# A two-layer hybrid backbone on one core: fold splits on VectorE, row copies first, the context's root inside the first product, and the order of the gate tiles

## The chip, the cores and the metric

The kernel runs on one core of a Trainium2 chip. The metric is the device time of one execution in microseconds, the median of several runs. A profile is one execution recorded by the hardware profiler; its span is the part of it between the first and the last instruction.

## The reference, cut to what matters

The network has two layers over 1024 latent tokens of width 1024; 256 context tokens only feed the recurrence of the first layer. The parts that the change touches stand at the very beginning of layer one, and in weights of layer two that are folded together ahead of time:

```python
shift, scale, gate = jnp.split(sc @ mod_w[l] + mod_b[l], 3, axis=-1)
hx = modulate(rmsnorm(x, norm_g[l]), shift[:, None], scale[:, None])
hc = modulate(rmsnorm(ctx, norm_g[l]), shift_c, scale_c)
...
xb_c = hc @ pe["w_in"][:, 3 * W_CONV:3 * W_CONV + W_LRU]
_, h_ctx = rglru_branch(xb_c, pe, h0, False)
out_x, _ = even_mixer(hx, h_ctx, pe)
```

`sc` is SiLU of the conditioning vector. `even_mixer` computes five products of `hx` (value va and gate vg of a convolution, ga, xb of the recurrence, gb). Layer two multiplies by a product of two weights (`od_w_in` and `od_w_grp`), which the kernel computes once: the "fold".

## The kernel before

All activations lie with channels on the 128 partitions, in eight tiles of 128 x 1024 (x_0 to x_7). Every product is made of float32r parts: an operand is split into a high part (a cast on ScalarE, "wh", "h0h", "cth") and a low part (source less high part, on VectorE or GpSimd, "wl", "h0l", "ctl"), and three matmuls replace one (high x high, high x low, low x high). `split` (line 102) and `wload` (line 123) do that for weights: a load into "wr", a cast into "wh", a subtraction into "wl", each with two buffers.

The beginning of the kernel, up to line 525, is one list of calls that is written out by hand. In it, loads (`load`, line 108) and matmuls (`mm`, line 117) are chained: each is issued after the one before it in the list. SP's queue thus takes the loads and the stores of the folds strictly in the written order, and a store that waits for its data holds back every load behind it. The other engines are ordered by a scheduler, within these chains and the data's dependences.

The list does these things, interleaved:

- `fold(g)` (line 250) for g = 0 and 1, as a generator that `fold_some` steps on. Each of its four parts takes a weight tile wu (through `weight`, line 254), makes 24 matmuls of 512 columns into two PSUM tiles, copies both into a tile fo on ScalarE, and puts a store of it on a list that `store_folds` (line 321) empties into SP's queue.
- The sum of squares of x, its root, spread over the partitions by a matmul (ms_x).
- The shift and scale of layer one, in four blocks b: `mod_loads` (line 374) multiplies four weight tiles (modw) by the conditioning into one PSUM row (modr), `mod_cols` (line 386) copies that row into SBUF on ScalarE (modrow) and turns it into columns by eight small matmuls (modt), which VectorE adds into m and a. `modulate(k)` (line 399) then scales tile x_k in place and splits it into h0h and h0l.
- The context: `ctx_load` (line 444) loads two tiles (cx) and sums their squares into ssqc, `ctx_scale` (line 452) takes the root (a matmul ms_c, a square root on ScalarE, a reciprocal on VectorE) and scales both tiles, `ctx_split` (line 458) modulates and splits them into cth and ctl.
- The gate of layer one: `spread_c` loads the conditioning onto all partitions (cL) and applies SiLU on ScalarE, and `gates(a, b)` (line 437) takes a weight tile each (mod) and forms its dot product with cL on VectorE.

Behind the list, the loop over j (line 770) runs the products of layer one in an order fixed by hand (`on`, line 530): xb_0 (lines 762 to 765, 48 matmuls, not chained to the list), then for j = 0 vg (48), the context's xbc (24 matmuls of 256 columns), va (48), the context's part for j = 1, and the recurrence's gate products g mixed with xb_1. The taps of a short convolution (uc), their split (uh, ul) and the products with the gates follow on VectorE, ScalarE and GpSimd. GpSimd makes the low parts of the weights in this loop (`raw_split`, line 565), after it has made those of three of the four tiles wu of fold 1.

Of the kernel before, what the change touches and what calls it, by code (L numbers as in the profile page):

```python
# [17 lines left out]
C = 256  # L18
E = C + S
D = 1024  # L20
KT = D // P
# [35 lines left out]
def body(ctx, tc, xT, ctxT, cc, ccol, modT, modW, win, gw, wout, wu, grp, wg, wo1, small, edge, ident, outT):  # L57
# [24 lines left out]
    def ttile(name):  # L82
        return tpool.tile([P, H], F32, tag="t", name=name)
# [8 lines left out]
    def wide(name):  # L92
        return pc.tile([P, S], F32, tag="xb", name=name)
# [33 lines left out]
    def wload(src, name, eng, n=D, out=None):  # L127
        raw = wpool.tile([P, n], F32, tag="wr", name=f"wr_{name}")
        load(raw, src)
        if out is None:  # L130
            hi = wpool.tile([P, n], F32R, tag="wh", name=f"wh_{name}")
            lo = wpool.tile([P, n], F32R, tag="wl", name=f"wl_{name}")
        else:
            hi, lo = out(f"wh_{name}", F32R), out(f"wl_{name}", F32R)
        split(raw, hi, lo, eng)
        return hi, lo


    def mm3_steps(ps, w, xs, cols, ks=KT):
        hi, lo = w  # L140
        xh, xl = xs
        for k in range(ks):
            kc = slice(k * P, (k + 1) * P)
            nc.tensor.matmul(ps, hi[:, kc], xh[k][:, cols], start=(k == 0), stop=False)  # L144
            nc.tensor.matmul(ps, hi[:, kc], xl[k][:, cols], start=False, stop=False)  # L145
            nc.tensor.matmul(ps, lo[:, kc], xh[k][:, cols], start=False, stop=(k == ks - 1))  # L146
            yield

    def mm3(ps, w, xs, cols, ks=KT):
# [48 lines left out]
    def rstd(acc, eps, name, wn=0):  # L198
        n = acc.shape[-1]
        ps = psum(f"ms_{name}") if n < H else banks(f"ms_{name}", wn)[0]  # L200
        nc.tensor.matmul(ps[:, :n], ones, acc, start=True, stop=True)
        rt = ttile(f"sq_{name}")
        nc.scalar.activation(rt[:, :n], ps[:, :n], AF.Sqrt, bias=eps)
        nc.vector.reciprocal(acc, rt[:, :n])
# [45 lines left out]
    def fold(g, raw_tile, out_tile, g_tile=None, w_tile=None):  # L250
        g_tile = g_tile or dtile
        gh, gl, early = [], [], None

        def weight(kp):
            return wload(wu[g, kp], f"wu_{g}_{kp}", nc.vector if g == 0 or kp == 0 else nc.gpsimd)

        for i in range(2):
            if w_tile is None and i == 1:
                early = weight(0)
            raw = raw_tile(f"graw_{g}_{i}")  # L260
            load(raw, grp[g, i])
            th = g_tile(f"gh_{g}_{i}", F32R)
            tl = g_tile(f"gl_{g}_{i}", F32R)
            split(raw, th, tl, nc.vector)
            gh += [th[:, 0:H], th[:, H:D]]
            gl += [tl[:, 0:H], tl[:, H:D]]
        yield
        if w_tile is not None:
            ws = [wload(wu[g, kp], f"wu_{g}_{kp}", nc.gpsimd, out=w_tile[kp]) for kp in range(KT // 2)]
            yield  # L270
        for kp in range(KT // 2):
            if w_tile is None:
                wh, wl = early
            else:
                wh, wl = ws[kp]
            if w_tile is None and kp + 1 < KT // 2:
                early = weight(kp + 1)
                yield
            pss = [psum(f"fold_{g}_{kp}_{s}") for s in range(2)]

            def terms(s):
                for i in range(4):
                    kc = slice(i * 2 * P + s * P, i * 2 * P + (s + 1) * P)
                    mm(pss[s], wh[:, kc], gh[i], start=(i == 0), stop=False)
                    mm(pss[s], wh[:, kc], gl[i], start=False, stop=False)
                    yield
                    mm(pss[s], wl[:, kc], gh[i], start=False, stop=(i == 3))
                    yield

            dst = wfold[g][:, :, 2 * kp : 2 * kp + 2, :]  # L290
            if w_tile is None:
                o = out_tile(f"fo_{g}_{kp}").rearrange("p (m s c) -> p m s c", s=2, c=P)
                todo = [terms(s) for s in range(2)]
                if (g, kp) == (0, 0):
                    for _ in range(2):
                        for t in todo:
                            for _ in range(4):
                                next(t)
                for s in range(2):
                    for _ in todo[s]:  # L300
                        pass
                    nc.scalar.copy(o[:, :, s, :], pss[s].rearrange("p (m c) -> p m c", c=P))
                    if s:
                        stores.append((dst.rearrange("m p s c -> p m (s c)"), o.rearrange("p m s c -> p m (s c)")))
                    yield
            else:
                for s in range(2):
                    for _ in terms(s):
                        pass
# [11 lines left out]
    def store_folds(n):  # L321
        while n and stores:
            load(*stores.pop(0))
            n -= 1
# [10 lines left out]
    with ExitStack() as sctx:  # L335
# [23 lines left out]
        def sumsq(acc_, v, n, first, name):  # L359
            if first:  # L360
                nc.scalar.activation(acc_[:, :n], v, AF.Square)
            else:
                q = ttile(name)
                nc.scalar.activation(q[:, :n], v, AF.Square)
                nc.vector.tensor_tensor(out=acc_[:, :n], in0=acc_[:, :n], in1=q[:, :n], op=add)


        idx = spool.tile([P, P], F32, name="idx")
# [5 lines left out]
        def mod_loads(b, qs):  # L374
            if b not in modr:
                modr[b] = psum(f"modr_{b}")
            for q in qs:
# [3 lines left out]
                for e in range(4):  # L381
                    mm(modr[b][32 * e : 32 * e + 32, j * MC : (j + 1) * MC], cpad[:, 4 * half + e],
                                     raw[:, e * MC : (e + 1) * MC], start=(q == 0), stop=(q == 3),
                                     skip_group_check=True)

        def mod_cols(b):
            row = ttile(f"modrow_{b}")
            nc.scalar.copy(row, modr[b])
# [55 lines left out]
        def ctx_load(i):  # L444
            cx.append(xtile(f"cx_{i}"))
            cth.append(ctile(f"cth{i}", F32R))
            ctl.append(ctile(f"ctl{i}", F32R))
            load(cx[i].rearrange("p (k n) -> p k n", n=C), ctxT[4 * i : 4 * i + 4].rearrange("k p n -> p k n"))
            for q4 in range(4):
                sumsq(accc, cx[i][:, q4 * C : (q4 + 1) * C], C, i + q4 == 0, f"csq_{i}_{q4}")  # L450

        def ctx_scale():
            rstd(accc, eps_r, "c")
# [30 lines left out]
        for _, roots in rx:  # L484
            roots()
        rx = [r for r, _ in rx]
        mod_cols(0)
        modulate(0)
        modulate(1)
        mod_loads(1, range(4))  # L490
        store_folds(2)
        fold_some(2)
        mod_cols(1)
# [1 line left out]
        modulate(3)  # L495
        fold_some(1)
        mod_loads(2, range(4))
        store_folds(1)
        fold_some(2)
        mod_cols(2)  # L500
        modulate(4)
        modulate(5)
        mod_loads(3, range(4))
        fold_some(1)
        mod_cols(3)
        modulate(6)
# [3 lines left out]
        fold_some(2)  # L510
        with tc.issue_after(last_low[0].ins), tc.issue_after(last_low[1].ins):
            ctx_load(0)
            ctx_load(1)
        w_vg0 = wload(win[KT], "vg0", nc.vector)
        store_folds(3)
        spread_c()
        gates(2 * KT, 2 * KT + 4)
        ctx_scale()
        ctx_split(0)
        ctx_split(1)  # L520
        raw_va0 = wpool.tile([P, D], F32, tag="wr", name="wr_va0")
        load(raw_va0, win[0])
        gates(2 * KT + 4, 2 * KT + 6)
        load(eg, edge)
        chained[0] = False


    last = {}

    def on(eng, f, *args, **kw):  # L530
        with ExitStack() as octx:
# [152 lines left out]
    with ExitStack() as actx:  # L684
# [77 lines left out]
        w = w_xb0  # L762
        xb = wide("xb0")
        for h in range(2):
            mm3(xb[:, HALF[h]], w, (hh, hl), HALF[h])
        xc = psum("xbc0")[:, :C]
        w = w_vg0
        uc = utile("uc0")
# [1095 lines left out]
```

## Time and profile before

| | |
|---|---|
| time, median of 3 runs | 1302.21 us (1300.24 to 1302.76) |
| the profiled execution | 1304.29 us, span 1302.4 us |
| mean granted TensorE clock | 0.991 |
| busy in the span: PE, DVE, ACT, POOL | 1268.6, 1135.5, 648.0, 296.3 us |
| PE busy from 60 to 70 us, and its clock | 8.72 of 10, 0.83 |
| PE busy from 90 to 100 us, and its clock | 6.32 of 10, 0.89 |
| PE busy from 100 to 110 us, and its clock | 9.60 of 10, 0.77 |

PE is TensorE's matmuls, PEld its weight loads, DVE is VectorE, ACT ScalarE, POOL GpSimd, SPq the queue that SP issues. A row of a timeline has the start, the length, the engine, the line, the operation, what it writes and reads, and in brackets the idle time of its engine ahead of it with what ended that. A row of a table by stretches has the stretch, its length, busy time and count of instructions of each engine, the granted clock, the share of time in which the DMA engines are busy, and GB/s.

### The profile page before, as it was taken

The numbers are of one execution on the slowest core, as the hardware profiler recorded it, in microseconds if no ns is written. First come the engines' busy times: TensorE is split into PE (matmuls) and PEld (weight loads), VectorE is DVE, ScalarE is ACT, GpSimd is POOL, SyncE is SP. The second block draws the span as 40 slices with busy tenths as digits, with TensorE's granted clock in tenths as the row PEclk, the third lists the DMA queues.
The fourth block names the chain that finished last, engine by engine and source line by source line (L and its number), as shares of the span: only waits on it lengthen the run. The fifth ranks groups of instructions, "written<-read, shape, count | busy, mean of one in ns | idle before, by whom it ended". The sixth has DMA issues, their size and how long they took to land.

```text
span 1302.4 us, 16089 instructions
## 1 busy us (share of the span) xinstructions
PE 1268.6 (97%) x5804; PEld 1042.2 (80%) x5804; DVE 1135.5 (87%) x1758; ACT 648.0 (50%) x937; POOL 296.3 (23%) x149
## 2 busy tenths in 40 slices
PE   9999999999999999999999999999999999999995
PEld 7678888888888887888887878887878888788784
DVE  6878899999999999968969969998999987887776
ACT  7543666566566633237535346633343434645442
POOL 0202644364535546443210022000000000000002
PEclk9998999999999999999999999999999999999997
DMA  9961111112111233442418565234333334868623
GB/s 367 385 212 41 57 54 53 57 57 73 39 67 57 70 127 120 156 143 90 155 40 298 172 209 175 93 122 154 120 115 114 113 121 141 295 226 278 227 78 129
DMA packets 78783, 182.33 MB, mean 140 GB/s; under 512 B 7664, under 2 KB 23408, under 8 KB 78704
## 3 DMA queue, kind: packets, MB, share of 16 engines
q1 hardware_dynamic: 70256, 177.12, 39.1%
q10 hardware_dynamic: 8448, 4.20, 1.1%
q8 instruction: 45, 0.74, 0.2%
q14 instruction: 34, 0.28, 0.1%
HBM read 137.24 MB, written 44.04 MB: 139 GB/s over the span
## 4 chain that ended last, share of the span: by engine, by line
PE 47%; DVE 29%; DMA 13%; ACT 4%; issue 4%; POOL 1%; SPq 0%; POOLq 0%; DVEq 0%; ACTq 0%
DVE conv L534 7%; PE wob L534 6%; PE va L534 5%; PE xb L534 4%; PE vg L534 4%; DVE l L534 3%; PE g L534 3%; DMA yr_t<-y_t 2%; DMA wr_wu<-wu 2%; PE ga L145 2%; PE ga L534 2%; PE ga L144 2%; PE ga L146 2%; PE xbc L534 2%; DVE ws L1401 1%
## 5 line engine op out<-in xcount | busy, mean ns | idle before, releaser
L534 DVE SCALAR_TENSOR_TENSOR conv<-u,sm,conv 128x505 f32<-128x505 f32 (+6 forms) x224 | 153.5, 745 | 1.0
L1683 POOL TENSOR_TENSOR o<-x,rr 128x256 f32<-128x256 f32 (+1 forms) x9 | 8.0, 927 | 454.0 <-ACT rr L1671 451.0
L534 ACT ACTIVATE l<-g,sm 128x512 f32<-128x512 f32 (+1 forms) x96 | 58.6, 618 | 57.8 <-PE g L534 57.0
L104 POOL TENSOR_TENSOR wl_wu<-wr_wu,wh_wu 128x1024 fp32r<-128x1024 f32 x11 | 26.3, 2393 | 160.0 <-ACT wh_wu L103 125.8
L123 PE MATMUL fold<-gh,wh_wu 128*128 128x512 f32 x128 | 51.7, 404 | 2.1 <-ACT wh_wu L103 2.1
L534 POOL TENSOR_TENSOR l<-l,l 128x1280 f32<-128x1280 f32 x16 | 47.1, 2962 | 25.6 <-DVE conv L534 14.0
L534 PE MATMUL wob<-ybl,wh_wob 128*128 128x512 f32 x128 | 50.1, 392 | 2.3 <-POOL ybl L534 2.3
L103 ACT CAST wq_g<-wr_g 128x512 fp32r<-128x512 f32 x48 | 28.2, 620 | 47.2 <-DMA wr_g<-wg 15.6
L123 PE MATMUL fold<-gh,wl_wu 128*128 128x512 f32 x128 | 50.7, 398 | 0.5 <-DVE wl_wu L104 0.5
L123 PE MATMUL fold<-gl,wh_wu 128*128 128x512 f32 x128 | 50.6, 395 | 0.2 <-DVE gl L104 0.2
L534 PE MATMUL va<-h0h,wh_va 128*128 128x512 f32 x128 | 50.2, 392 | 0.0
L534 PE MATMUL gb<-h0h,wl_gb 128*128 128x512 f32 x128 | 49.9, 390 | 0.2 <-POOL wl_gb L534 0.2
L534 PE MATMUL va<-h0l,wh_va 128*128 128x512 f32 x128 | 50.0, 391 | 0.0
L534 PE MATMUL va<-h0h,wl_va 128*128 128x512 f32 x128 | 50.0, 391 | 0.0
L534 PE MATMUL wob<-ybh,wl_wob 128*128 128x512 f32 x128 | 49.8, 389 | 0.0
L534 PE MATMUL gb<-h0h,wh_gb 128*128 128x512 f32 x128 | 49.8, 389 | 0.0
L534 PE MATMUL gb<-h0l,wh_gb 128*128 128x512 f32 x128 | 49.8, 389 | 0.0
L534 PE MATMUL vg<-h0h,wl_vg 128*128 128x512 f32 x128 | 49.8, 389 | 0.0
L534 PE MATMUL vg<-h0l,wh_vg 128*128 128x512 f32 x128 | 49.8, 389 | 0.0
L534 PE MATMUL wob<-ybh,wh_wob 128*128 128x512 f32 x128 | 49.8, 389 | 0.0
L534 PE MATMUL vg<-h0h,wh_vg 128*128 128x512 f32 x128 | 49.8, 389 | 0.0
L534 DVE TENSOR_TENSOR_SCAN l<-l,l 128x256 f32<-128x256 f32 (+1 forms) x32 | 48.7, 1522 | 1.1
(593 smaller groups left out, 4303.8 us busy)
## 6 DMA issues: line engine op xcount, KB each, us to landing
wr_wu<-wu SPq DMA_DIRECT2D x16, 512.0 KB, 4.9
modw<-modW SPq DMA_DIRECT2D x16, 512.0 KB, 10.2
x_part<-xp SPq DMA_DIRECT2D x32, 256.0 KB, 2.2
mod<-modT SPq DMA_DIRECT2D x32, 256.0 KB, 3.8
wr_v<-wfold SPq DMA_DIRECT2D x16, 512.0 KB, 4.0
wr_g<-wg SPq DMA_DIRECT2D x16, 512.0 KB, 5.0
wr_wo<-wo SPq DMA_DIRECT2D x16, 512.0 KB, 4.7
yr_t<-y_t SPq DMA_DIRECT2D x16, 512.0 KB, 6.2
```

The source lines that it names most:

```text
L103: return (nc.scalar.copy(hi, src), eng.tensor_tensor(out=lo, in0=src, in1=hi.bitcast(F32), op=sub))
L104: eng.tensor_tensor(out=lo, in0=src, in1=hi.bitcast(F32), op=sub))
L123: m = nc.tensor.matmul(*args, **kw)
L144: nc.tensor.matmul(ps, hi[:, kc], xh[k][:, cols], start=(k == 0), stop=False)
L145: nc.tensor.matmul(ps, hi[:, kc], xl[k][:, cols], start=False, stop=False)
L146: nc.tensor.matmul(ps, lo[:, kc], xh[k][:, cols], start=False, stop=(k == ks - 1))
L534: last[eng] = f(*args, **kw)
L1401: nc.vector.tensor_tensor(out=nxt[:, :, a_:b_], in0=cur[:, :, a_ + o0 : b_ + o0], in1=cur[:, :, a_ + o1 : b_ + o1], op=add)
L1683: nc.gpsimd.tensor_tensor(out=o[:, k - k0], in0=v, in1=rr, op=mult)
```

## The change

Five edits, all in the first 110 us of the kernel. The three low parts of fold 1's weights move from GpSimd to VectorE. The row copy of `mod_cols` gets a call of its own (`mod_row`), which stands right behind its matmuls; for block 3 it is also put ahead of `modulate(4)`. In the list, one of the three last stores of the folds goes behind the conditioning, two gate tiles and va's weight. Two of the six gate products stand ahead of the context's root, bound behind its last sum of squares, and four behind the last split of the context. And xb_0 is now chained to the list: its first 12 of 16 steps stand ahead of the root's matmul, 4 behind it.

```diff
         def weight(kp):
-            return wload(wu[g, kp], f"wu_{g}_{kp}", nc.vector if g == 0 or kp == 0 else nc.gpsimd)
+            return wload(wu[g, kp], f"wu_{g}_{kp}", nc.vector)
...
+        rows = {}
+
+        def mod_row(b):
+            rows[b] = ttile(f"modrow_{b}")
+            return nc.scalar.copy(rows[b], modr[b])
+
         def mod_cols(b):
-            row = ttile(f"modrow_{b}")
-            nc.scalar.copy(row, modr[b])
+            row = rows[b]
...
         mod_cols(2)
-        modulate(4)
+        mod_loads(3, range(4))
+        with tc.issue_after(mod_row(3).ins):
+            modulate(4)
         modulate(5)
-        mod_loads(3, range(4))
...
             ctx_load(0)
-            ctx_load(1)
+            squares = ctx_load(1)
         w_vg0 = wload(win[KT], "vg0", nc.vector)
-        store_folds(3)
+        store_folds(2)
         spread_c()
-        gates(2 * KT, 2 * KT + 4)
-        ctx_scale()
-        ctx_split(0)
-        ctx_split(1)
+        with tc.issue_after(squares.ins):
+            gates(2 * KT, 2 * KT + 2)
         raw_va0 = wpool.tile([P, D], F32, tag="wr", name="wr_va0")
         load(raw_va0, win[0])
-        gates(2 * KT + 4, 2 * KT + 6)
+        store_folds(1)
+        xb0 = wide("xb0")
+        first = (x for h in range(2) for x in mm3_steps(xb0[:, HALF[h]], w_xb0, (hh, hl), HALF[h], KT, mm))
+        for _ in range(KT + 4):
+            next(first)
+        ctx_scale()
+        for _ in first:
+            pass
+        ctx_split(0)
+        with tc.issue_after(ctx_split(1)[1].ins):
+            gates(2 * KT + 2, 2 * KT + 6)
         load(eg, edge)
         chained[0] = False
 
-    last = {}
+    last = {"pe": pe[0]}
```

The same is done in `rstd` (its matmul goes through `mm`), and lines 762 to 765 go.

On ScalarE, around the row copy of block 3 (modrow of modr_699 before, of modr_687 now); h0h_689 and h0h_716 are the high part of x_4, the next one that of x_5, wh_xb the cast of xb_0's weight. Before:

```order
L103 COPY wh_wu_3_656<-wr_wu_3_654 128x1024
L302 COPY fo_2_662<-fold_2_0_660 128x4x128
L406 ACTIVATE h0h_689<-x_290,m_132 128x1024
L406 ACTIVATE h0h_695<-x_412,m_132 128x1024
L388 COPY modrow_737<-modr_699 128x512
L103 COPY wh_xb_762<-wr_xb_760 128x1024
```

And now:

```order
L103 COPY wh_wu_3_658<-wr_wu_3_656 128x1024
L302 COPY fo_2_664<-fold_2_0_662 128x4x128
L390 COPY modrow_712<-modr_687 128x512
L411 ACTIVATE h0h_716<-x_290,m_132 128x1024
L411 ACTIVATE h0h_722<-x_412,m_132 128x1024
L103 COPY wh_xb_762<-wr_xb_760 128x1024
```

The row copy moved ahead of both high parts.

On VectorE, from the last sum of squares of the context to its second low part ctl_812; mod_16 and the following are the gate tiles, uc the first tap behind xb_0. Before:

```order
L365 TENSOR_TENSOR ssqc<-ssqc,csq_3_823 128x256
L441 TENSOR_SCALAR mod_16_837,m_132<-mod_16_837,cL 128x1024
L441 TENSOR_SCALAR mod_17_840,m_132<-mod_17_840,cL 128x1024
L204 RECIPROCAL ssqc<-sq_c 128x256
L441 TENSOR_SCALAR mod_18_843,m_132<-mod_18_843,cL 128x1024
L441 TENSOR_SCALAR mod_19_846,m_132<-mod_19_846,cL 128x1024
L456 TENSOR_TENSOR cx_796<-cx_796,ssqc 128x1024
L456 TENSOR_TENSOR cx_810<-cx_810,ssqc 128x1024
L441 TENSOR_SCALAR mod_20_870,m_132<-mod_20_870,cL 128x1024
L415 TENSOR_SCALAR cx_796<-cx_796,a_133,m_132 128x256 x4
L441 TENSOR_SCALAR mod_21_873,m_132<-mod_21_873,cL 128x1024
L415 TENSOR_SCALAR cx_810<-cx_810,a_133,m_132 128x256 x4
```

And now, from the second gate product on:

```order
L446 TENSOR_SCALAR mod_17_839,m_132<-mod_17_839,cL 128x1024
L204 RECIPROCAL ssqc<-sq_c 128x256
L463 TENSOR_TENSOR cx_796<-cx_796,ssqc 128x1024
L463 TENSOR_TENSOR cx_810<-cx_810,ssqc 128x1024
L420 TENSOR_SCALAR cx_796<-cx_796,a_133,m_132 128x256 x4
L420 TENSOR_SCALAR cx_810<-cx_810,a_133,m_132 128x256 x4
L104 TENSOR_TENSOR ctl_798<-cx_796,cth_797 128x1024
L104 TENSOR_TENSOR ctl_812<-cx_810,cth_811 128x1024
L446 TENSOR_SCALAR mod_18_913,m_132<-mod_18_913,cL 128x1024
L446 TENSOR_SCALAR mod_19_916,m_132<-mod_19_916,cL 128x1024
L446 TENSOR_SCALAR mod_20_919,m_132<-mod_20_919,cL 128x1024
L446 TENSOR_SCALAR mod_21_922,m_132<-mod_21_922,cL 128x1024
```

Four gate products left the context's chain and stand between it and the taps uc.

On ScalarE, the end of the context's chain: csq are its squares, cL the conditioning's SiLU, cth the high parts, wh_va the cast of va's weight. Now:

```order
L302 COPY fo_3_769<-fold_3_1_768 128x4x128
L103 COPY wh_vg_828<-wr_vg_826 128x1024
L440 ACT_TABLE_LOAD
L440 ACTIVATE cL<-cL 128x1024
L364 ACTIVATE csq_1_817<-cx_810 128x256
L364 ACTIVATE csq_2_820<-cx_810 128x256
L364 ACTIVATE csq_3_823<-cx_810 128x256
L203 ACT_TABLE_LOAD
L203 ACTIVATE sq_c<-ms_c,eps_r 128x256
L103 COPY cth_797<-cx_796 128x1024
L103 COPY cth_811<-cx_810 128x1024
L553 COPY wh_va_975<-wr_va_842 128x1024
```

Before, cL and its table load stood behind the last three squares, and wh_va, a convolution tap, a table load and a sigmoid stood between the two cth.

More of the change, by code (lines that the diff above doesn't have):

```diff
@@ L136, in wload, with mm3_steps @@
         return hi, lo
-    def mm3_steps(ps, w, xs, cols, ks=KT):
+    def mm3_steps(ps, w, xs, cols, ks=KT, mm=nc.tensor.matmul):
         hi, lo = w
@@ L143, in mm3_steps @@
             kc = slice(k * P, (k + 1) * P)
-            nc.tensor.matmul(ps, hi[:, kc], xh[k][:, cols], start=(k == 0), stop=False)
-            nc.tensor.matmul(ps, hi[:, kc], xl[k][:, cols], start=False, stop=False)
-            nc.tensor.matmul(ps, lo[:, kc], xh[k][:, cols], start=False, stop=(k == ks - 1))
+            mm(ps, hi[:, kc], xh[k][:, cols], start=(k == 0), stop=False)
+            mm(ps, hi[:, kc], xl[k][:, cols], start=False, stop=False)
+            mm(ps, lo[:, kc], xh[k][:, cols], start=False, stop=(k == ks - 1))
             yield
@@ L200, in rstd @@
         ps = psum(f"ms_{name}") if n < H else banks(f"ms_{name}", wn)[0]
-        nc.tensor.matmul(ps[:, :n], ones, acc, start=True, stop=True)
+        mm(ps[:, :n], ones, acc, start=True, stop=True)
         rt = ttile(f"sq_{name}")
@@ L364, in sumsq @@
                 nc.scalar.activation(q[:, :n], v, AF.Square)
-                nc.vector.tensor_tensor(out=acc_[:, :n], in0=acc_[:, :n], in1=q[:, :n], op=add)
+                return nc.vector.tensor_tensor(out=acc_[:, :n], in0=acc_[:, :n], in1=q[:, :n], op=add)
         idx = spool.tile([P, P], F32, name="idx")
@@ L449, in ctx_load @@
             for q4 in range(4):
-                sumsq(accc, cx[i][:, q4 * C : (q4 + 1) * C], C, i + q4 == 0, f"csq_{i}_{q4}")
+                d = sumsq(accc, cx[i][:, q4 * C : (q4 + 1) * C], C, i + q4 == 0, f"csq_{i}_{q4}")
+            return d
         def ctx_scale():
@@ L486, in body @@
         rx = [r for r, _ in rx]
+        mod_row(0)
         mod_cols(0)
@@ L490, in body @@
         mod_loads(1, range(4))
+        mod_row(1)
         store_folds(2)
@@ L497, in body @@
         mod_loads(2, range(4))
+        mod_row(2)
         store_folds(1)
@@ L760, in gate_steps @@
                         yield
[L762 to L765, printed above, removed]
+        xb = xb0
         xc = psum("xbc0")[:, :C]
```

## The prediction

> **What bounds the kernel now.** I read the page's slices first, then a table by stretches of the beginning, the waits of PE there, and the timelines engine by engine. TensorE is busy nearly everywhere; only near 62 and 97 us do busy time and granted clock dip. The table's columns are stretch, length, then busy time and count of PE, PEld, DVE, ACT, POOL, then granted clock, DMA share and GB/s.
>
> ```profile
> 60.21:63.62 3.41, 2.13 (x13) 1.55 (x12) 3.39 (x4) 3.25 (x4) 0.00 (x0) 1.00 0.98 346
> 63.62:67.04 3.42, 3.42 (x11) 2.84 (x11) 2.90 (x8) 0.71 (x2) 0.00 (x0) 0.50 0.61 209
> 67.04:70.45 3.41, 3.41 (x16) 2.78 (x16) 1.69 (x4) 1.95 (x3) 0.00 (x0) 1.00 0.00 0
> 90.93:94.35 3.42, 2.61 (x13) 1.83 (x11) 3.42 (x9) 1.20 (x2) 0.00 (x0) 1.00 0.70 252
> 94.35:97.76 3.41, 1.30 (x9) 1.10 (x10) 3.41 (x6) 3.38 (x4) 2.54 (x1) 1.00 0.15 60
> 97.76:101.17 3.41, 2.26 (x9) 1.67 (x8) 2.17 (x3) 1.33 (x2) 1.17 (x1) 0.50 0.27 77
> 101.17:104.59 3.42, 3.42 (x14) 3.07 (x13) 2.45 (x4) 0.56 (x1) 0.00 (x0) 0.50 0.00 0
> ```
>
> After PE was busy for only 2.13, 1.30 and 2.26 of 3.41 us, the next stretch ran at half clock; after 2.61 it did not. So the two waiting places cost more than their waits. The waits of PE up to 130 us name what it waited for (total, times, longest):
>
> ```profile
> PE xbc L534 <- DVE ctl L104: 2.8, 2, 2.1
> PE xbc L534 <- ACT cth L103: 1.3, 2, 0.8
> PE modt L123 <- ACT modrow L388: 1.3, 1, 1.3
> ```
>
> PE's timeline (start, length) shows what lies between:
>
> ```profile
> 61.28 0.39 PE L123 MATMUL fold<-gh,wl_wu 128*128 128x512 f32 x1
> 62.95 1.28 PE L123 MATMUL modt<-sm,modrow 128*128 128x2 f32 x8 [1.28 <-ACT modrow L388]
> 64.09 0.77 PE L123 MATMUL fold<-gh,wh_wu 128*128 128x512 f32 x1
> ...
> 71.04 0.39 PE L144 MATMUL xb<-h0h,wh_xb 128*128 128x512 f32 x1
> ...
> 82.35 0.39 PE L534 MATMUL vg<-h0h,wh_vg 128*128 128x512 f32 x1
> ...
> 104.61 0.40 PE L534 MATMUL va<-h0l,wh_va 128*128 128x512 f32 x1
> ...
> 114.61 0.28 PE L534 MATMUL xbc<-cth,wh_xb 128*128 128x256 f32 x1
> 114.72 0.28 PE L534 MATMUL xbc<-ctl,wh_xb 128*128 128x256 f32 x1
> ```
>
> At full clock a 512-column matmul starts every 0.227 us (44 of va from 104.61 to 114.61), a 256-column one every 0.12. 104.61 is va's fifth, so a va that is never slowed would have started at 103.70. From there the waits of PE show none up to 420 us, so what is won before va is won for the program, if nothing else becomes late.
>
> **The change, step by step.** First the three fold splits (wl_wu) that go from GpSimd to VectorE. Rows of POOL's and of DVE's timeline:
>
> ```profile
> 48.03 2.40 POOL L104 TENSOR_TENSOR wl_wu<-wr_wu,wh_wu 128x1024 fp32r<-128x1024 f32 x1 [11.05 <-ACT wh_wu L103]
> 48.42 2.10 DVE L242 SCALAR_TENSOR_TENSOR a<-m,sm 128x2 f32<-128x2 f32 x2
> 56.90 1.66 DVE L242 SCALAR_TENSOR_TENSOR a<-m,sm 128x2 f32<-128x2 f32 x2
> 64.41 1.22 DVE L104 TENSOR_TENSOR wl_xb<-wr_xb,wh_xb 128x1024 fp32r<-128x1024 f32 x1
> 65.55 0.23 DVE L242 SCALAR_TENSOR_TENSOR a<-m,sm 128x2 f32<-128x2 f32 x2
> ```
>
> A pair of 2-column operations takes 2.10 us while GpSimd's split runs, 1.66 beside the next split, and 0.23 without one. The same split is 1.22 on VectorE. So the move costs 1.22 a time and frees 1.9 and 1.4: x_2 and x_3 are scaled 0.9 us earlier (the 0.7 net, and 0.2 of idle ahead of the pair), and x_4 at 57.1 instead of 58.5, since there PE's dot products for its scale come at 56.6 as before and the split fits ahead of them. The third split, near 35 us, stands ahead of work that waits for PE anyway: nothing. The Trainium skill, "SBUF — State Buffer", section "Who interferes with whom", says that a VectorE instruction with two SBUF inputs and a GpSimd instruction that reads SBUF shut each other out for a whole instruction; 2.10 us beside 0.23 agrees.
>
> Then the row copy (modrow) and the queue of loads, rows of ACT and SP:
>
> ```profile
> 62.33 0.57 ACT L388 COPY modrow<-modr 128x512 f32<-128x512 f32 x1
> 58.88 15.64 SPq L113 DMA_DIRECT2D wfold<-fo  x3
> 74.57 0.50 SPq L113 DMA_DIRECT2D cL<-cc  x1
> cL<-cc SPq DMA_DIRECT2D x1, 512.0 KB, 5.9
> ```
>
> Now that copy stands ahead of h0h_4 and h0h_5, directly behind its dot products on PE (58.7). It ends at 59.3 and holds h0h_4 back to there, which is still 0.7 earlier than before, since x_4 came 1.4 earlier. So modt runs right at the fold's end, 61.50. The fold followed modt's start by 1.14 us, of which 0.47 lay in the half-clock stretch: 0.9 at full clock. It starts at 62.40, not 64.09, and its 24 matmuls (5.44 us) bring xb to **67.84 instead of 71.04**: 3.2 us, half of it clock. Cover: xb's first matmul needs the last scaling of x_7 off its PSUM bank, by my sum at 66.95, 0.9 ahead.
>
> The context's root is next. ScalarE's and VectorE's rows between the sum of squares and xbc's operands:
>
> ```profile
> 71.39 1.33 ACT L364 ACTIVATE csq<-cx 128x256 f32<-128x256 f32 x4
> 80.46 1.06 ACT L435 ACTIVATE cL<-cL 128x1024 f32<-128x1024 f32 x1 [4.10 <-DMA cL<-cc]
> 82.36 1.28 ACT L203 ACT_TABLE_LOAD   x1 [0.84 <-PE ms_c L201]
> 84.42 1.75 DVE L204 RECIPROCAL ssqc<-sq_c 128x256 f32<-128x256 f32 x1
> 86.08 1.17 DVE L441 SCALAR_TENSOR_TENSOR mod<-mod,cL 128x1024 f32<-128x1024 f32 x1
> 99.12 1.23 DVE L104 TENSOR_TENSOR ctl<-cx,cth 128x1024 fp32r<-128x1024 f32 x1 [1.24 <-ACT cth L103]
> ```
>
> SP's three stores ended at 74.5, because the third waits for the last fold's copy, and held back cL and every gate tile. Now only two stand ahead: cL is issued near 63.4 and, at 5.9 us, lands at 69.3. ScalarE ends h0h_7 at 68.1, does five squares (0.33 each), the fold's copy and vg's cast until 71.1, table load and cL until 73.45, three squares until 74.5; VectorE adds the last at 75.3. PE asks for the sum after 36 of xb's 48 matmuls, at 67.84 + 8.15 = 76.0: **0.7 us of cover**. The next table load no longer waits for PE and is over before PE's result. Two dots (1.15 each) end at 77.6; the reciprocal takes 1.65, the scaling of both tiles 2.3, two modulations 1.3 each, then the casts: ctl_1 is ready near 87.3, 11 us after the root's matmul, where it took 18 (82.3 to 100.3). Gone from between are a table load (1.28), two dots behind the reciprocal and two behind the scaling (4.6), and the ScalarE instructions that stood ahead of the second cast.
>
> PE: vg starts 11.31 after xb as now (82.35 - 71.04), at 79.15; its 48 matmuls end at 90.02; xbc (24 x 0.12) finds its operands 2.7 us old and runs to 92.89. That is **10.8 us before 103.70**.
>
> What is late next is va's weight. In the built program its cast takes the buffer of vg's weight, so it can't begin before PE's last reads of that (89.95), whatever else moves; ScalarE ends it at 91.0, then GpSimd splits it:
>
> ```profile
> 95.22 3.71 POOL L534 TENSOR_TENSOR wl_va<-wr_va,wh_va 128x1024 fp32r<-128x1024 f32 x1 [36.75 <-ACT wh_va L534]
> 136.77 1.28 DVE L534 SCALAR_TENSOR_TENSOR uc<-xb,sm,uc 128x1022 f32<-128x1022 f32 x1 [2.96 <-ACT uc L534]
> ```
>
> Until now xbc's waits hid that split. Now va's third matmul wants it at 93.34. Bounds: a split of 2.40, as at 48.03, ends at 93.5 (stall 0.2), one of 3.71 at 94.8 (stall 1.5). The last of the four moved dots is running when it starts, until 91.9, and the 3.71 row is itself 2.33 behind the end of a VectorE split (96.60), so I take 91.9 + 2.33 = 94.25: **a stall of 0.9**. Queued behind this split on GpSimd are those of xb_1's and the gate weight; I get their ends at 103.5 and 105.8, and PE wants them at 105.2 and 107.8. VectorE, now with four dots ahead of its taps, ends ul near 100 and u near 107.2, which PE wants at 107.7 and 110. Its 2.96 us of idle at 136.77 shows it waiting for PE in that round, so its lag of 1.7 behind PE's gain dissolves there. The last store, va's load and the other gate tiles move to where the table shows DMA at 0.61 and 0.00: nothing. Sum: 10.8 - 0.9 = **9.9 us**.
>
> **Rivals.** *Half clock stays somewhere.* A stall of 0.9 leaves 2.5 us busy of 3.41; 2.61 kept full clock, 2.26 (itself at half clock) did not. One half-clock stretch costs 1.7: gain 8.2. Nor need these stretches lie the same in every execution, so the stall may fall across two. The Trainium skill, "TensorE: Matmul & The Clock Gate", section "HAM oscillation — how this bites in real kernels", warns of idle gaps above some 3.4 us; by that the stall would touch no clock and 9.9 would stand, but here a gap of 1.28 was followed by 0.50, so the rows decide.
>
> *Nothing won.* VectorE carries the chain of waits for long after 332 us. Were it filled from 110 on without idle, its own head start would rule there, and one wait at xb or ms_c could take that back. Against it stands the idle of 2.96.
>
> *Slower.* The root's matmul now stands within xb, and its sum waits behind cL on ScalarE: all of PE hangs on one load. It needs cL by 72.4 and has 0.7 more; from 73.1 on each microsecond goes to the end, with about two half-clock stretches (3.4). From a landing near 79.7 the change loses; at 82.5, 19 us after issue, the time is some 1305 to 1307. Against it: 5.9 us to landing so far, and a DMA share that falls from 0.98 to 0.61 just then.
>
> **How the numbers follow.** The profiled execution took 1304.3 (span 1302.4), 2.1 above the median of the three runs and 1.5 above the highest. 9.9 off it gives 1294.4. If the 2.1 belong to profiling, the runs give 1292.3; if they are half-clock stretches that other executions miss, part of the gain is in those already and 1294.4 stays. I take the middle, 1293.3. Chances: forecast 0.67, half clock 0.21 (1295.0), nothing won 0.07 (about 1301), slower 0.05. Low end: 1292.3 less 0.7 (smallest stall) and about 1 for the spread of runs, 1290.5. High end: 1294.4 with one half-clock stretch and 1 us at ms_c, 1297.1. A measurement of this kernel tells about 0.2% (2.6 us) from no change: faster 0.88, same 0.07, slower 0.05.
>
> **What would show it.** No idle ahead of modt; xb starting near 67.8; cL issued between 63 and 64; ms_c without idle; xbc without idle; 0.2 to 1.5 us of idle at va's third matmul, released by GpSimd's wl_va; clock 1.00 from 60 to 105; every 2-column pair of VectorE at 0.23. An idle above 1 us at ms_c, or half clock at va, would make the prediction too low; new waits of PE behind 110 us would refute the part on what follows.

## The result

The changed kernel took 1293.47 us in the median of 6 runs (1293.18 to 1298.71), beside 1303.0 us for the kernel before in the same set (6 runs, 1300.24 to 1305.87): a ratio of 0.9937 [0.9916, 0.9957], which here is that of the two means (the two medians alone give 0.9927). The prediction was 1293.3 us. The profiled execution took 1293.43 us with a span of 1291.6, which is 10.8 us less than the span of before; the forecast for that difference was 9.9.

First the waits of PE in the first 130 us of the changed kernel. Those for modrow, cth and ctl are gone; the three left lie ahead of 35 us.

```profile
PE warm L123 <- DVE ones L161: 1.1, 1, 1.1
PE fold L123 <- DVE wl_wu L104: 0.5, 1, 0.5
PE fold L123 <- ACT wh_wu L103: 0.2, 1, 0.2
```

The table by stretches (columns as in the prediction) at the two places where PE stood still or ran at half clock before:

```profile
60.00:70.00 10.00, 10.00 (x49) 8.36 (x49) 9.75 (x16) 7.56 (x13) 0.00 (x0) 1.00 1.01 344
...
90.00:100.00 10.00, 9.90 (x54) 8.31 (x54) 7.36 (x10) 6.88 (x9) 2.40 (x2) 1.00 0.08 26
100.00:110.00 10.00, 10.00 (x59) 8.81 (x58) 9.93 (x15) 2.12 (x5) 5.63 (x2) 1.00 0.30 107
```

PE was busy 10.00, 9.90 and 10.00 us of each 10, at clock 1.00, where it had been 8.72, 6.32 and 9.60 at 0.83, 0.89 and 0.77. PE's timeline of the changed kernel at the steps of the prediction:

```profile
60.97 0.95 PE L123 MATMUL modt<-sm,modrow 128*128 128x2 f32 x8
...
67.36 0.39 PE L123 MATMUL xb<-h0h,wh_xb 128*128 128x512 f32 x1
...
75.52 0.59 PE L123 MATMUL ms_c<-ssqc,ones 128*128 128x256 f32 x2
...
78.71 0.39 PE L553 MATMUL vg<-h0h,wh_vg 128*128 128x512 f32 x1
...
89.59 0.28 PE L553 MATMUL xbc<-cth,wh_xb 128*128 128x256 f32 x1
...
92.47 0.40 PE L553 MATMUL va<-h0h,wh_va 128*128 128x512 f32 x1
92.70 0.40 PE L553 MATMUL va<-h0l,wh_va 128*128 128x512 f32 x1
93.20 0.50 PE L553 MATMUL va<-h0h,wl_va 128*128 128x512 f32 x1
```

None of these rows has a bracket, so PE waited at none of them. Only va's third matmul starts 0.50 us behind the second instead of 0.23: a stall of 0.27, too short for the list of waits. What they hang on, from the timelines of DVE, ACT, SP and POOL of the changed kernel:

```profile
49.03 0.24 DVE L242 SCALAR_TENSOR_TENSOR a<-m,sm 128x2 f32<-128x2 f32 x2
...
56.51 0.23 DVE L242 SCALAR_TENSOR_TENSOR a<-m,sm 128x2 f32<-128x2 f32 x2
58.21 0.59 ACT L390 COPY modrow<-modr 128x512 f32<-128x512 f32 x1 [2.17 <-PE modr L123]
62.96 0.50 SPq L113 DMA_DIRECT2D cL<-cc  x1
73.32 1.49 DVE L365 TENSOR_TENSOR ssqc<-ssqc,csq 128x256 f32<-128x256 f32 x3 [1.26 <-ACT csq L364]
76.15 0.47 ACT L203 ACTIVATE sq_c<-ms_c,eps_r 128x256 f32<-128x256 f32 x1 [0.95 <-PE ms_c L123]
83.66 2.43 DVE L104 TENSOR_TENSOR ctl<-cx,cth 128x1024 fp32r<-128x1024 f32 x2
89.45 1.22 DVE L446 SCALAR_TENSOR_TENSOR mod<-mod,cL 128x1024 f32<-128x1024 f32 x1
90.74 2.40 POOL L553 TENSOR_TENSOR wl_va<-wr_va,wh_va 128x1024 fp32r<-128x1024 f32 x1 [90.30 <-DVE mod L446]
```

The 2-column pairs take 0.24 and 0.23 us, the row copy runs directly behind its dot products, cL is issued at 62.96 instead of 74.57, the last sum of squares is there at 74.8, 0.7 ahead of ms_c, and the low parts of the context at 86.1, 3.5 ahead of xbc. The bracket of wl_va names a gate product because that ended last, at 90.67; the cast of va's weight, which the split reads, had ended at 90.66.

### The profile page after: what moved, and what is told of

Same layout as the page of the kernel before. It is cut to its first block, busy times and chain, and to the rows that moved or that the text cites. A ratio compares the mean times of both kernels' runs of the same rounds, so it can differ in the third digit from the quotient of the medians.

```text
span 1291.6 us, 16081 instructions
## 1 busy us (share of the span) xinstructions
PE 1263.2 (98%) x5804; PEld 1039.1 (80%) x5804; DVE 1134.7 (88%) x1761; ACT 647.6 (50%) x937; POOL 287.5 (22%) x146
## 4 chain that ended last, share of the span: by engine, by line
PE 48%; DVE 31%; DMA 13%; issue 4%; ACT 3%; POOL 1%; SPq 0%; POOLq 0%; DVEq 0%; ACTq 0%
DVE conv L553 7%; PE wob L553 6%; PE vg L553 5%; PE va L553 5%; PE xb L553 4%; PE fold L123 3%; DVE l L553 3%; PE g L553 3%; DVE ws L1417 2%; DMA wr_v<-wfold 2%; DMA yr_t<-y_t 2%; PE ga L553 2%; PE ga L146 2%; PE ga L145 2%; PE ga L144 2%
## 5 line engine op out<-in xcount | busy, mean ns | idle before, releaser
L103 ACT CAST wq_v<-wr_v 128x512 fp32r<-128x512 f32 x48 | 28.1, 620 | 44.1 <-DMA wr_v<-wfold 18.5
## 6 DMA issues: line engine op xcount, KB each, us to landing
modw<-modW SPq DMA_DIRECT2D x16, 512.0 KB, 10.2
```

The lines of the kernel that those rows point to most:

```text
L103: return (nc.scalar.copy(hi, src), eng.tensor_tensor(out=lo, in0=src, in1=hi.bitcast(F32), op=sub))
```

## Experiments

Twelve runs, in three sets; the kernel before took 1305.4, 1306.5 and 1305.05 us there, so only ratios are compared across sets. They can't order kernels that differ by one edit, since most intervals are 2 to 3 us to either side. The traces can, by a **mark**: the start of va's last matmul, behind which every kernel has the same work. From the mark to the end of the span it was 1188.0 us in before, 1188.1 in after, and 1187.8 to 1192.7 in the other twelve, less the waits behind the mark that the table names. Waits behind 115 us (12.6 to 16.1 us in all) and, in three of the traces, half-clock stretches behind 700 us make up much of that scatter. It is not the edits': the two traces of the changed kernel alone lie 4.5 us apart there.

| kernel | mark, us | PE's waits, 55 to 112 us | half clock there, us | ratio to before |
|---|---|---|---|---|
| before | 114.38 | 5.4 | 10.2 | 1 |
| after | 103.53 | 0.3 | 0 | 0.9937 [0.9916, 0.9957] |
| after_again | 103.48 | 0.3 | 0 | 0.9927 [0.9909, 0.9946] |
| front_half | 110.46 | 3.9 | 6.8 | 0.9981 [0.9965, 0.9997] |
| back_half | 105.94 | 2.4 | 0 | 0.9936 [0.992, 0.9951] |
| splits_back | 104.33 | 0.6 | 0 | 0.9908 [0.9893, 0.9923] |
| row_back | 104.68 | 0.9 | 0 | 0.993 [0.9913, 0.9946] |
| store_back | 103.58 | 0.3, and 3.6 behind it | 3.4 behind it | 0.9938 [0.9917, 0.9959] |
| dots_back | 109.76 | 3.2 | 6.8 | 0.9947 [0.9927, 0.9968] |
| root_last | 104.46 | 1.1, and 1.6 behind it | 0 | 0.9943 [0.9924, 0.9962] |
| root_at_8 | 107.33 | 2.0 | 3.4 | 0.9938 [0.9918, 0.9959] |
| one_dot | 104.04 | 0.7 | 0 | 0.9928 [0.9907, 0.9949] |
| late_root | 110.22 | 4.6 | 6.8 | 0.9975 [0.9965, 0.9985] |
| va_low_on_dve | 103.06 | 0 | 0 | 0.9935 [0.992, 0.9951] |

The 0.3 of after and after_again is the stall at va's third matmul, counted from start to start; dots_back, root_at_8 and late_root have it too, beside what the table gives. A half-clock stretch costs half of the time that PE is busy in it: 4.5 us of the mark of before, 2.9 in front_half, 3.1 in dots_back, 1.7 in root_at_8 and 2.2 in late_root. Each kernel but the changed one has a single trace, so how often other executions pay this is not shown.

**after_again**, the changed kernel once more, as a control.

> The changed kernel once more, as the control of the three others on one chip, since the time of the kernel before was 1303.0, 1305.4 and 1306.5 us in three sets of runs. Waits theory: va ends near 103.5 us, no wait of PE from 60 to 112 us above 0.3 us, no half clock there, and a ratio inside 0.9916 to 0.9957. Rival, that part of the first ratio was that one set of runs: ratio above 0.996.

The mark came 0.05 us from that of the first trace, and the ratio 0.001 from the first. The gain is no matter of one set of runs.

### One half of the change at a time

**front_half** is the kernel before with the splits on VectorE and the row copies moved, nothing else:

```diff
-            return wload(wu[g, kp], f"wu_{g}_{kp}", nc.vector if g == 0 or kp == 0 else nc.gpsimd)
+            return wload(wu[g, kp], f"wu_{g}_{kp}", nc.vector)
...
         mod_cols(2)
-        modulate(4)
+        mod_loads(3, range(4))
+        with tc.issue_after(mod_row(3).ins):
+            modulate(4)
         modulate(5)
-        mod_loads(3, range(4))
```

> The kernel before with the splits on VectorE and the row copies first, nothing else. Waits theory (PE's two waiting places, each with its half clock, are the whole gain): the wait at modt goes and xb starts some 3 us earlier, but cL still waits for the last fold's store, so the context is ready only as much earlier as that store, about 2.6 us; the waits and the half clock at xbc stay. Span 2.5 to 3 us below the kernel before. VectorE theory (the time freed on VectorE by GpSimd's splits carries the gain): nearly all of it, 7 us or more, is there.

xb started at 67.17, as in after, but PE then waited for the context as before, and the clock fell again. The waits of PE up to 130 us, and the table on the clock's own grid:

```profile
PE xbc L543 <- DVE ctl L104: 2.8, 2, 2.1
PE xbc L543 <- ACT cth L103: 1.1, 2, 0.8
```

```profile
87.54:90.95 3.41, 2.41 (x10) 1.51 (x9) 3.41 (x10) 2.20 (x3) 0.12 (x1) 1.00 0.74 296
90.95:94.36 3.41, 1.56 (x11) 1.36 (x11) 2.53 (x3) 3.38 (x4) 3.41 (x1) 1.00 0.00 0
94.36:97.78 3.42, 2.36 (x9) 2.07 (x10) 3.02 (x3) 0.33 (x1) 0.17 (x1) 0.50 0.22 77
97.78:101.19 3.41, 3.41 (x12) 2.83 (x12) 2.13 (x4) 0.79 (x2) 0.00 (x0) 0.50 0.00 0
```

What the front saves arrives (3.9 us at the mark, some 0.4 of it there before the first edit; 2.5 us by the ratio; 2.5 to 3 were expected), and the back's waits stay what they were.

**back_half** is the changed kernel with those two edits taken out (the diff above, read the other way).

> The kernel before with the store moved, two dots ahead and four behind, and the root inside xb; splits on GpSimd and the row copy behind h0h_5. Waits theory: modt still waits some 1.3 us and one half-clock stretch may follow, xbc no longer waits: 7 to 8 us below the kernel before, 3 above the changed kernel. VectorE theory: at most 2 us below the kernel before.

The mark came 8.4 us earlier than before, where 7 to 8 were expected. The ratio, 0.9936, is that of the whole change: the 2.4 us between the two marks don't show in it. Two waits are left, modt's for its row copy and va's for its low part:

```profile
PE modt L123 <- ACT modrow L388: 1.6, 1, 1.6
PE va L544 <- POOL wl_va L544: 0.9, 1, 0.9
```

The halves add up to 12.4, the whole is 10.85. One reason is the 0.4 us of the start, which is in both halves. Another is the clock: this wait of 1.6 us was longer than that of before (1.28), and no half clock followed, because it fell across two stretches:

```profile
58.43:61.84 3.41, 2.54 (x12) 1.75 (x10) 3.41 (x5) 2.13 (x2) 0.00 (x0) 1.00 1.06 356
61.84:65.25 3.41, 2.71 (x16) 2.42 (x17) 3.09 (x8) 2.08 (x4) 0.00 (x0) 1.00 0.59 210
```

The half clock at 63.6 in the trace of before thus hung on where the grid lay in that execution, and not on the wait alone.

**splits_back** and **row_back** undo one of these two edits each: the first has the condition `g == 0 or kp == 0` again, the second puts the row copy back into `mod_cols`, behind `modulate(4)` and `modulate(5)`.

> The changed kernel with the three splits back on GpSimd. Waits theory: the pairs take 2.1 and 1.7 us again and x_4 comes 1.4 later, but the row copy still stands first, so modt doesn't wait; xb waits 0.4 for the last scaling, the root's sum has no cover left, va's split may meet a dot: 0.5 to 1.5 us above the changed kernel. VectorE theory: 5 us or more above it.

> The changed kernel with the row copy back behind h0h_5. Waits theory: with the splits on VectorE h0h_5 ends at 60.5 and the copy at 61.0, when PE comes to modt (60.97): 0 to 0.3 us above the changed kernel, so that splits and row copy stand in for each other at this wait. Rival (the row copy alone removed the wait): modt waits 1.3 us again, with half clock 3 us above.

In splits_back the pairs of 2-column operations are slow again (the second took 1.69), but modt doesn't wait:

```profile
48.05 2.09 DVE L242 SCALAR_TENSOR_TENSOR a<-m,sm 128x2 f32<-128x2 f32 x2
```

xb started at 67.62 without the splits and at 67.75 without the row copy; with both it was 67.36, with neither 69.00. The two edits are nearly substitutes at this place: of the 1.64 us that they win together, either one alone wins 1.25 or more, and the second only adds the rest. The marks are 0.85 us (splits_back) and 1.2 us (row_back) behind the control's. The first is as expected; of the second I had expected 0 to 0.3. There xb is 0.45 late, the gate products end at 91.97 instead of 90.57, and GpSimd's split of va's weight meets the last of them, takes 3.15 and lets PE wait 0.85: the delay that modt doesn't show comes back behind it.

### The parts of the back

**store_back** has all three stores ahead of cL again:

```diff
-        store_folds(2)
+        store_folds(3)
         spread_c()
...
         load(raw_va0, win[0])
-        store_folds(1)
```

> The changed kernel with the third store ahead of cL again. cL is issued near 70 and lands at 76; in this build the last squares stand ahead of cL on ScalarE, so the root's matmul doesn't wait, but its square root stands behind cL and a table load: ctl_1 comes near 89.4, still ahead of xbc. Waits theory: PE's new wait is behind that, at va or at the context part of j = 1, because the four dots run until 94, GpSimd's split of va's weight cuts in, and the taps start 4 us late: 3 to 6 us above the changed kernel. Rival (only xbc's operands matter): no more than 1 us above.

The squares stood ahead of cL, PE never waited at ms_c, and the mark is that of after. The delay came out behind it. VectorE's and GpSimd's rows, and PE's next waits:

```profile
90.85 3.42 DVE L446 SCALAR_TENSOR_TENSOR mod<-mod,cL 128x1024 f32<-128x1024 f32 x1
...
96.50 3.91 DVE L552 SCALAR_TENSOR_TENSOR uc<-xb,sm,uc 128x1022 f32<-128x1022 f32 x3
104.68 3.36 POOL L552 TENSOR_TENSOR wl_xb<-wr_xb,wh_xb 128x1024 fp32r<-128x1024 f32 x1 [11.49 <-ACT wh_xb L552]
104.66 0.38 PE L552 MATMUL xbc<-cth,wh_xb 128*128 128x256 f32 x1 [0.69 <-ACT wh_xb L552]
108.09 0.58 PE L552 MATMUL xbc<-cth,wl_xb 128*128 128x256 f32 x1 [2.94 <-POOL wl_xb L552]
```

The gate products ran 3.7 us later, one of them was shut out by wl_va's split (3.42 instead of 1.22), the taps started at 96.50 instead of 91.80, and at the end of that line xb_1's weight was late by 3.6 us on PE, with a half-clock stretch behind. By the start of the next vg the trace is 5.6 us behind the control's (130.01, 124.43), within the 3 to 6 expected and at one of the two places named, the context part of j = 1. The ratio doesn't show it. What the earlier cL buys is VectorE's head start, not only the root.

**late_root** makes the root hang on cL, as the prediction's slower rival has it and store_back doesn't: three stores first, `ctx_load` as two functions (the load `ctx_tile`, the sums `ctx_squares`), and the second context tile's squares held behind cL.

```diff
-            ctx_load(0)
-            squares = ctx_load(1)
+            ctx_tile(0)
+            ctx_squares(0)
+            ctx_tile(1)
...
-        store_folds(2)
-        spread_c()
+        store_folds(3)
+        silu = spread_c()
+        with tc.issue_after(silu.ins):
+            squares = ctx_squares(1)
...
         load(raw_va0, win[0])
-        store_folds(1)
```

> Three stores of folds ahead of cL again, and the four squares of the second context tile held behind cL's SiLU on ScalarE, so that the root hangs on that load as the prediction's slower rival has it. In the earlier run with three stores ahead cL landed at 75.8 us. By the rival's price (from 73.1 us on each microsecond of landing goes to the end, and two half-clock stretches come with it): a wait of 2.7 to 3.4 us at ms_c, 1.7 to 3.4 us of half clock, va's end at 108 to 110.4 us, and a ratio of 0.996 to 0.9985. Other view, that PE's matmuls behind it make room: wait below 1 us, va's end below 105.

ScalarE's row gives cL's landing, PE's the wait:

```profile
76.55 1.06 ACT L440 ACTIVATE cL<-cL 128x1024 f32<-128x1024 f32 x1 [5.06 <-DMA cL<-cc]
```

```profile
80.10 1.19 PE L123 MATMUL ms_c<-ssqc,ones 128*128 128x256 f32 x2 [4.58 <-DVE ssqc L365]
```

By the price of the prediction's slower rival a landing at 76.55 costs 76.55 - 73.1 = 3.4 us and two half-clock stretches (3.4), 6.8 in all. The mark came 6.7 us behind after_again's, and the ratio is 0.0048 above it, 6.3 us. The rival's mechanism is right, but its terms are not, and that their sum fits is luck. PE waited 4.58 us, above the 2.7 to 3.4 expected: it asked 0.5 us earlier than forecast, and four squares and sums stood behind cL instead of three. The two half-clock stretches cost 2.2 us and not 3.4, because PE still waited in the first and was busy for only 0.96 us of it:

```profile
77.65:81.06 3.41, 0.96 (x3) 0.84 (x3) 2.80 (x7) 2.46 (x5) 0.00 (x0) 0.50 1.03 418
```

In the changed kernel the rival's condition, a landing near 79.7, wasn't met by far.

**dots_back** lets the gate products stand where the scheduler puts them:

```diff
-        with tc.issue_after(squares.ins):
-            gates(2 * KT, 2 * KT + 2)
+        gates(2 * KT, 2 * KT + 4)
...
-        with tc.issue_after(ctx_split(1)[1].ins):
-            gates(2 * KT + 2, 2 * KT + 6)
+        ctx_split(1)
+        gates(2 * KT + 4, 2 * KT + 6)
```

> The changed kernel with the dots in the old calls, free of bounds: three of them now lie between the last sums of squares. Waits theory: the sum is ready at 77.7 instead of 74.8, PE waits 2.2 us inside xb, ctl_1 comes at 90.2 before PE needs it: 2 us above the changed kernel, 3.7 with one half-clock stretch. Rival (the dots' place does nothing): 0.

The mark was 6.2 us later, far more than I expected (2, or 3.7 with one half-clock stretch). VectorE now took four gate products ahead of and between the last sums of squares, so that the last of these started at 78.18:

```profile
78.18 0.42 DVE L365 TENSOR_TENSOR ssqc<-ssqc,csq 128x256 f32<-128x256 f32 x1
```

PE waited 3.19 us at ms_c and ran at half clock for 6.8 (3.1 lost). With the root inside xb, the products' place behind the sums is, in this trace, a condition of the gain.

**root_last** and **root_at_8** move the root's matmul from behind 12 of xb's 16 steps to behind all 16, and to behind 8 (`range(KT + 4)` becomes `range(2 * KT)`, and `range(KT)`).

> The changed kernel with the root's matmul behind all 16 steps of xb. It comes 2.7 us later and ctl_1 near 88.7, still ahead of xbc (89.6). Waits theory with the chain behind it: dots until 93.3 or, with GpSimd's split cutting in, 95.6; the taps, uh, and xb_1's weight split come up to 3.8 us late, and the context part of j = 1 waits: 0.4 to 4 us above the changed kernel. Rival (xbc's operands alone count): 0.

> The changed kernel with the root's matmul after 8 of the 16 steps. PE comes to it at 72.8, the sum is ready at 74.8: PE waits 2.0 us there and nothing else moves. Waits theory: 2.0 us above the changed kernel, 3.7 with one half-clock stretch behind it. Rival (the earlier root brings the context earlier and wins): 0 or below.

At 8 PE asks 2.0 us too early, and a half-clock stretch follows: 3.85 us at the mark, as expected with one stretch. At 16 PE doesn't wait at ms_c or xbc, but the gate products come 2.3 us later and meet wl_va's split:

```profile
90.67 3.38 POOL L553 TENSOR_TENSOR wl_va<-wr_va,wh_va 128x1024 fp32r<-128x1024 f32 x1 [90.23 <-ACT wh_va L553]
91.76 3.38 DVE L446 SCALAR_TENSOR_TENSOR mod<-mod,cL 128x1024 f32<-128x1024 f32 x1
```

The split waits for the product that was running, the next product for the split. PE waits 1.08 at va and 1.60 at xb_1's context part, and the next vg starts 2.8 us later than in the control (127.27, 124.43), within the 0.4 to 4 expected. Of the three places, 12 steps is the best by the traces: the sum is 0.7 us early, and the products are out of the split's way.

The four ratios of this set (0.9938 to 0.9947) show less than the marks do: dots_back's 6.2 us would be 0.0048, and it lies 0.0010 to 0.0020 above after. The kernel before was at its slowest in this set (up to 1311.5 us), and the control didn't run in it. The traced execution of dots_back was also the slowest of its six (1302.75 us, the others 1297.93 to 1301.72). How much of these losses reaches the median is open; for late_root, beside its control, nearly all of it did.

### The stall at va

**one_dot** has one gate product ahead of the root and five behind (`2 * KT + 2` becomes `2 * KT + 1`, twice).

> One gate product ahead of the root and five behind, in place of two and four. The last product then ends near 91.5 us instead of 90.6, behind the end of wh_va's cast (90.7). Theory, that GpSimd's split takes 2.40 us only if no VectorE instruction that reads two SBUF operands runs beside it: the split takes 3.1 to 3.4 us and PE waits 0.8 to 1.2 us at va's third matmul, so va ends at 104.1 to 104.5 us. Rival, that the split's 0.27 us is what the cast sets: split 2.4, wait 0.3, va's end unchanged. The time differs from the control's by less than 0.1 per cent either way.

The split started 0.64 us ahead of the end of the last product (91.28, where VectorE's next instruction starts) and took 0.58 more:

```profile
90.14 1.22 DVE L446 SCALAR_TENSOR_TENSOR mod<-mod,cL 128x1024 f32<-128x1024 f32 x1
90.64 2.98 POOL L553 TENSOR_TENSOR wl_va<-wr_va,wh_va 128x1024 fp32r<-128x1024 f32 x1 [90.19 <-ACT wh_va L553]
93.67 0.50 PE L553 MATMUL va<-h0h,wl_va 128*128 128x512 f32 x1 [0.68 <-POOL wl_va L553]
```

By the list PE waited 0.68. From first to last start va took 11.68 us, in the control 11.07, and 10.68 in va_low_on_dve, where nothing holds it: 1.0 lost here and 0.4 in the control. That is the theory's side, not the rival's (split 2.4, wait 0.3), but short of its ranges: the split was expected at 3.1 to 3.4, the wait at 0.8 to 1.2, the mark from 104.1 on. The split takes 2.40 plus the rest of the VectorE instruction that it meets, less 0.06 to 0.10: 2.67 in splits_back (0.34 of rest), 2.98 here (0.64), 3.38 in root_last (1.08). Those of store_back, row_back and back_half fit as well (2.56, 3.15 and 3.17 with 0.22, 0.83 and 0.84).

**va_low_on_dve** makes that low part on VectorE, behind the fourth product:

```diff
-                wva = raw_split(raw_va0, "va0")
+                wva = raw_split(raw_va0, "va0", nc.vector.tensor_tensor)
```

> The low part of va's weight on VectorE, behind the fourth of the moved gate products, instead of GpSimd. Theory: it starts with the cast's end at 90.7 us, takes 1.22, and is there at 91.9, a full microsecond before PE asks: no wait at va, va ends 0.2 to 0.3 us earlier than in the control; the taps uc, which wait for ScalarE until 91.8, start at most 0.2 us later, and PE does not see it. Time equal to the control's within 0.1 per cent. Rival: the taps' delay comes back as a wait of PE at xb_1's or the gate's products behind 103 us.

```profile
90.60 1.23 DVE L588 TENSOR_TENSOR wl_va<-wr_va,wh_va 128x1024 fp32r<-128x1024 f32 x1
91.75 3.91 DVE L553 SCALAR_TENSOR_TENSOR uc<-xb,sm,uc 128x1022 f32<-128x1022 f32 x3
```

No wait at va, the taps not later than in after, and the mark 0.42 us ahead of the control's. That is the best beginning of all kernels here, but the total doesn't show it: 0.9935 [0.992, 0.9951] beside 0.9927 [0.9909, 0.9946]. Nor is splits_back's 0.9908 a better kernel, with its mark 0.8 us later. No version is shown to be faster than the changed kernel.

## Why the prediction was right, step by step

- **Splits on VectorE.** As forecast: both pairs at 0.23 to 0.24. That GpSimd's split beside them is the cause is shown by splits_back, where the pairs took 2.09 and 1.69 again.
- **Row copy, xb.** Forecast 67.84, measured 67.36. Of the difference 0.35 were there at 37 us already (the second modr at 36.92 instead of 37.27; at 36.83 and 36.86 in front_half and back_half, so no edit made it). The 3.2 us held against this trace of before, but half of them were half clock, which hung on the grid of that execution (back_half).
- **The context's root.** The cover of 0.7 us at ms_c was exact. ctl came at 86.1 instead of 87.3: 0.4 is the earlier start, and 0.8 I lost by laying both casts behind all modulations, while the first runs beside those of the second tile. xbc found its operands 3.5 us old (forecast 2.7).
- **The head start of va.** Forecast 10.8 against an unslowed start at 103.70; measured 103.70 - 92.47 = 11.2, of which 0.4 is the start of the execution.
- **The stall at va was the mis-sized term**: 0.9 forecast, 0.27 measured at that matmul (0.4 by va's last). The rule was right (2.33 behind the end of the VectorE instruction that runs; 2.29 to 2.34 in splits_back, one_dot and root_last), its input wasn't: the last product ended at 90.6, not at 91.9, for the reasons under the context's root. So it was past when the cast ended, and the split ran in 2.40.
- **Behind va.** No wait of PE from there to 420 us. GpSimd's splits ended at 103.4 and 105.6 (103.5 and 105.8), u was there at 106.9 (107.2).
- **From trace to median.** The span fell by 10.8, the ratio says 8.2 us (0.9937 of 1302.21). I had taken the middle between two readings of the 2.1 us by which before's profiled execution lay above the median. That the number fits to 0.2 us is luck in this step: the two ratios of one kernel already differ by 1.3 us, and 4.5 of the 10.85 us at the mark are half clock of one execution of before.
- **Rivals.** There was no half clock from 5 to 1278 us of the trace, so "half clock stays" didn't come, and I gave it too much: by the stretches below, one with a stall of 0.9 (2.5 us busy) was in no danger. "Nothing won" is refuted by the waits up to 420 us. "Slower" had its mechanism right and its sum by luck (late_root).

## What to carry to other kernels

Where two engines shut each other out, place the work so that neither is running when the other's short or urgent instruction comes; the price is the rest of the other's instruction, and it is paid by whoever waits at the end of that line (products, taps, a weight, TensorE). When a root or a sum is moved into a long product, work out its cover in both directions: in the traces four steps earlier cost 3.9 us here (1.7 of it half clock), four later 2.8. And undo one edit at a time: two edits that each look like the cause may be substitutes.

## What the runs showed of the hardware

The clock changes on a grid of 3.41 us that begins elsewhere in each execution (full clock first granted 4.3 to 7.2 us behind the start). Over the fourteen traces, at full clock, each stretch with PE busy for 1.56 us or less was followed by half clock, and none with 1.58 or more (over a hundred between 1.58 and 2.7), but for three. One is before's at 60.21 with 2.13, of which 0.67 us were the 2-column matmuls of modt. The others stand at the program's end, at 1277.97 in after_again with 1.73 and at 1277.45 in va_low_on_dve with 1.84, of which 0.61 each were 1-column matmuls (fin_ms). Without these tiny matmuls they have 1.46, 1.12 and 1.23, which fits, and counted so no full-clock stretch of the fourteen traces falls on the wrong side; no run tried it by itself. Two traces show rows from either side of that bound, after_again first, then row_back:

```profile
714.77:718.18 3.41, 1.48 (x7) 0.89 (x6) 3.41 (x9) 1.68 (x4) 0.00 (x0) 1.00 0.76 261
718.18:721.60 3.42, 3.42 (x10) 2.68 (x9) 3.42 (x10) 0.62 (x1) 0.00 (x0) 0.50 0.66 212
```

```profile
717.14:720.55 3.41, 1.58 (x7) 1.31 (x8) 3.30 (x8) 1.62 (x3) 0.00 (x0) 1.00 0.72 249
720.55:723.97 3.42, 3.42 (x17) 2.83 (x16) 3.42 (x12) 0.62 (x1) 0.00 (x0) 1.00 0.67 207
```

It is the same place in the program, with nearly the same wait; where the grid fell decided. The way back asks for more: at half clock, stretches with 2.36 (front_half) and 2.75 us busy (dots_back) were followed by half clock again, those with 2.96 (store_back) and more by full:

```profile
78.08:81.49 3.41, 2.75 (x7) 2.21 (x8) 1.52 (x4) 0.48 (x1) 0.00 (x0) 0.50 0.46 181
81.49:84.91 3.42, 3.42 (x10) 2.65 (x9) 3.42 (x5) 0.00 (x0) 0.00 (x0) 0.50 0.02 5
```

```profile
107.65:111.06 3.41, 2.96 (x14) 2.97 (x15) 3.38 (x5) 0.00 (x0) 2.60 (x2) 0.50 0.42 153
```

The Trainium skill, "TensorE: Matmul & The Clock Gate", section "What's actually happening", calls the window free-running with 3413 ns, and these traces agree. Its section "HAM oscillation — how this bites in real kernels" warns of gaps above some 3.4 us; here 1.9 us of idle time within one stretch were enough, and the measurement decides. A wait of 2 us can cost 1.7 more or nothing, by chance, and this is part of why the runs of one kernel differ by several microseconds: 1.7 of the 4.5 us between the two traces of the changed kernel.
